# A two-layer hybrid block: the mLSTM value projection as seven products of quarters, with 4 KB slots and a matmul order that groups 128-column matmuls

## The chip, the cores and the metric

The kernel runs on one core of a Trainium2 chip. The metric is the device time of one execution in microseconds (us); lower is better. Five engines matter: TensorE (PE in the profile, its weight loads are PEld), VectorE (DVE), ScalarE (ACT), GpSimd (POOL), and SyncE (SP), which here only issues transfers.

## The reference, cut to what matters

Two layers of this (512 tokens, model width 1024, float32):

```python
h = rmsnorm(x, norm_g)
proj = h @ w_in            # aq, ak, av, az, bqk, bv, bi, bf, bo, bz, ga, gb
oa = diff_attention(rope(norm(aq)), rope(norm(ak)), av, lam)
ya = (rmsnorm(oa) * silu(az)) @ w_out_a
qk = silu(causal_conv(bqk))
hb = mlstm(q, k, bv, i_pre, f_pre)        # 8 heads, values 128 wide
yb = (sigmoid(bo) * rmsnorm(hb) * silu(bz)) @ w_out_b
u = sigmoid(ga) * ya + sigmoid(gb) * yb
x = x + u @ w_o
```

The piece changed most is `bv = h @ w_bv`, a product of 512 x 1024 by 1024 x 1024, whose result the mLSTM heads use as values.

## The kernel before

**Numbers.** Every float32 operand is cut in two: hi, rounded to the type that TensorE takes, and lo, the rest. ScalarE writes hi and VectorE subtracts to get lo (`split`). A product is three matmuls (`mm3`): hi by hi, hi by lo, lo by hi. `hh` and `hl` are hi and lo of the normalised input, transposed, resident for the whole layer.

**Pieces.** The weights come in pieces of 128 x 1024 (512 KB). For each, SP's queue loads `wr` (two buffers), `prep` splits it into `wh` and `wl` (three buffers each), and TensorE runs 24 matmuls of 512 columns. A token piece (qk, av, bv; `tok_piece`) adds into four accumulators, one for each 128 tokens; four pieces finish half the columns. A feature piece (az, bqk, bo, bz, ga, gb, woa, wob; `feat_piece`) finishes 128 columns in one accumulator. PSUM has four accumulators (`ps_acc`), a double one for scores (`ps_sc`), and one each for transposes and for head outputs. `TUNE["order"]` is the hand-written order of pieces.

**Seven products.** The output projection wo already runs as seven products of quarters (`seven`): both matrices are cut into 2 x 2 quarters, the products P1 to P7 take sums of quarters as operands, and their results are joined. A product is two pieces of 12 matmuls. Three accumulator pairs are used: X for P1, P6, P7, P4; Y for P5, P3; Z (the score accumulator) for P2. The sums on the weight side are made by loading one quarter on SP's queue and adding others in with accumulating transfers on POOL's queue (`add_up`). The sums on the other side are made from the gated rows by VectorE (`u_forms`).

**Heads.** Around these pieces, eight attention heads and eight mLSTM heads a layer run as chains of steps (`attn_head`, `ml_head`), timed in units of a quarter piece by offsets in TUNE. They need VectorE and ScalarE for masks, exponentials, norms and splits, and TensorE for scores, transposes and value products.

**The planner.** All instructions are first recorded, then `Recorder.schedule` orders them by a model of each engine: at each step the engine that can start earliest takes the candidate with the lowest key. A key is a due time, worked back from the order of TensorE's work, with offsets by tile name (`bias`), `slack`, `margin`, and penalties such as `drain`; `pemargin` is an extra delay before TensorE may use what another engine wrote. SP keeps program order. The result is a fixed order for each engine's queue; every queue runs in that order, and an instruction that waits holds those behind it.

**Memory.** Slots of 4 KB a partition (`qkp`, tag q2, 20 of them; `take` and `give` count them) hold hi-lo pairs, sums and forms. Besides, a 16 KB tile `big` holds in turn x, the q and k of attention groups 0 and 2, and `ua`.

Of the kernel before, what the change touches and what calls it, by code (L numbers as in the profile page):

```python
# [42 lines left out]
    ),  # L43
    "qkt": 5,
    "gct": 15,
    "gls": 6,
    "glf": 5,
    "attn": (1, 5, 5, 8, 9, 13, 15, 16, 19, 24),
    "a0": 23,
    "ap": 18,  # L50
    "a4": 7,
    "ml": (1, 9, 11, 12, 13, 28),
    "ahead": 3,
    "lc": 7,
    "slack": 4956.0,
    "margin": 72.0,
    "pemargin": 206.2,
    "wait": 333.1,
    "swpen": 141896579.9,
    "smargin": 51.6,  # L60
    "pwait": 0.7,
    "wdiff": 3673.3,
# [9 lines left out]
    "acl": 14,  # L72
    "gateA": 9,
    "gateM": 4,
    "actp": (0, 2, 3),
    "m0": 217,
    "mp": 15,
    "m4": 9,
    "slots": 20,
    "bias": {'av': 30400.0, 'msp_a': -4350.0, 'wl': 2200.0, 'wo': -3700.0, 'woh': -4650.0, 'ht': 29250.0, 'taz': -4050.0, 'ga': 25150.0, 'gt': -8800.0, 'p': -900.0, 'wo1_P': 27550.0, 'out_0_dram': -5850.0, 'p5_wo': -4950.0, 'rot': 12400.0, 'dq': -4400.0, 'oa': 450.0, 'dd': 31000.0, 'num': 20100.0, 'ld': -7300.0, 'ws1_wo': -2200.0, 'gw': -1100.0, 'hl': -600.0, 'sc': -1500.0, 'uz': -3750.0, 'mk': 7950.0, 'sbz': 4200.0, 'az': 12900.0, 'posi': 3200.0, 'msl_d': 1650.0, 's1_wo': 5000.0, 'msh_d': 6450.0, 'sq': -1400.0, 'warm': 3150.0, 'bo': -450.0, 'sdl': 150.0, 'ml': 16100.0, 'fo_b': 12850.0, 'ws0_wo': -900.0, 'wt1_wo': 1400.0, 'pb': 8800.0, 'sbo': 5350.0, 'qkt': 3900.0, 'junk': 7400.0, 'ulZ': 6400.0, 'bv': 650.0, 'bqk': -1750.0, 'uh': -3950.0, 'ms_b': -1100.0, 'ob': -400.0, 'uy': 1500.0, 'ms': 11100.0, 'ms_a': 1750.0, 'ones': 4150.0, 'msh_b': 8300.0, 'x1d': -3000.0, 'saz': 1000.0, 'xr': -3950.0, 'wo0_P': 450.0, 'qk1_0x': 2050.0, 'msh_a': 6050.0, 'rnh': -3150.0, 'gft': 6600.0, 'gct': 3100.0, 'kl': -700.0, 'qk1_2x': -800.0, 'gf': 1550.0, 'qk0_0x': -1600.0, 'qy': 7250.0, 'msl_a': 1400.0, 'x': -4550.0, 'eps': -600.0, 'wt0_wo': -2500.0, 'xn': 400.0, 'msl_b': 2150.0, 'rn': -400.0, 'glf': -3500.0, 'ss': 7600.0, 'sinv': 6150.0, 'ulA': -2650.0, 'epsc': -3000.0, 'ulB': 950.0, 'ulY': -300.0, 'tbz': 350.0, 'hh': 3700.0, 'fo_a': 6500.0, 'mx': -1800.0, 'gc': -150.0, 'mq': -1050.0, 'ang': 3150.0, 'qt': -2500.0, 'uhZ': -1250.0, 'em': -6800.0, 'ct': 1000.0, 'fo_d': 3850.0, 'par': -250.0, 'ks': 250.0, 'den': -400.0, 'sdh': -1000.0, 'cv': -300.0, 'ng': 3750.0, 'uhB': 300.0, 'rows': -300.0, 'zw': 50.0, 'qs': 1350.0, 'ctab': 950.0, 'gcol': 3400.0, 'ul': 1000.0, 'fb_b': 400.0, 'sums': 400.0, 'cosv': 250.0},  # L80
    "drain": 467.1,
    "risk": 268.4,
    "late": 912.7,
# [18 lines left out]

class Recorder:
# [3 lines left out]
    ACT_SET = {"Exp": (0, 6), "Tanh": (0,), "Ln": (6,), "Sin": (9,)}  # L107
    SET_NAME = {0: "exp_and_others", 6: "natural_log_exp_and_others", 9: "trig_and_small"}
# [56 lines left out]
    def add(self, eng, e, fn, a, k):  # L165
# [49 lines left out]
        self.ops.append({"eng": eng, "e": e, "fn": fn, "a": a, "k": k, "pre": preds, "cost": cost, "nom": self.pe_time, "rows": rows, "kind": a[0].tensor.name.rstrip("_0123456789")})  # L215
# [56 lines left out]
    def schedule(self):  # L272
# [48 lines left out]
        at_rows = {"ACT": (0, 0), "DVE": (0, 0)}  # L321

# [15 lines left out]
        while len(order) < n:  # L338
# [42 lines left out]
            if e in at_rows:  # L381
                if o["rows"] != at_rows[e]:
                    s = max(s, free[e] + 115.0)
                at_rows[e] = o["rows"]
            if e == "ACT":
# [59 lines left out]
def kernel(ctx, tc, x, pos, wp, wg, cst, par, pb, ngb, out):  # L445
# [53 lines left out]
    xcur = big.tile([P, NT, D], F32, tag="big", name="x0")  # L499
# [76 lines left out]
    state = {"x": [xcur[:, tt, :] for tt in range(NT)], "t": 0, "n": 0, "q2": 1}  # L576
# [9 lines left out]
    def run_due():  # L586
        fn = heapq.heappop(due)[2]
        if fn() is False:
            at(state["t"] + 1, fn)
# [36 lines left out]
    def layer_events(l):  # L626
        lam_init = 0.8 - 0.6 * math.exp(-0.3 * l)
        par_l = pt[l]
        st = {}
        xres = x if l == 0 else x1d  # L630
# [3 lines left out]
        def layer_consts():  # L634
# [26 lines left out]
            gc = cp.tile([P, 2], F32, tag=f"gc{l}", name=f"gc{l}")  # L661
            V.tensor_scalar(gc[:, 0:1], par_l[:, G_AN : G_AN + 1], 0.25 * (1.0 - lam_init), None, ALU.mult)
            V.tensor_scalar(gc[:, 1:2], par_l[:, G_MN : G_MN + 1], 0.125, None, ALU.mult)
            st["gc"] = gc


# [15 lines left out]
        def norm_scale(tt):  # L682
# [6 lines left out]
            if l:  # L689
                give(1)  # L690

        def norm_back(tt):
            if tt == NT - 1:
                give(1)
            junk = st[("junk", tt)]
            for hf in range(2):
# [8 lines left out]
                )  # L705

# [53 lines left out]
        CHAIN = {"P1": "X", "P6": "X", "P7": "X", "P4": "X", "P5": "Y", "P3": "Y", "P2": "Z"}  # L760
        LEFT = {"P1": "A00", "P2": "A01", "P3": "S4", "P4": "A11", "P5": "S1", "P6": "S2", "P7": "S3"}

        def seven(name, lhs, out, over):
            loc = {}
            seq = TUNE["prods"].split()

            def post(prod, t):
# [15 lines left out]
                elif prod == max("P3", "P6", key=seq.index):  # L783
                    out(0, 1, t, Y[t], X[t])
# [7 lines left out]
            def piece(prod, a):  # L792
                def run(wh, wl):
                    c = CHAIN[prod]
                    first = prod in ("P1", "P5", "P2")
                    if first and a == 0:
                        if prod == "P2":

                            z = ps_sc.tile([P, 2, S], F32, tag="sc", name=f"{name}{l}_{prod}")
# [12 lines left out]
                    if a == 1:  # L812
                        over(prod)
# [17 lines left out]

        def qk_done(c, tt, acc):
            if tt == 0:
                names = ("qs0", "qs1", "ks0", "ks1")
                if c % 2 == 0:
                    until(lambda: c == 0 or st.get(("A", 1), 0) > 5)
                    xt = big.tile([P, 8, S], F32R, tag="big", name=f"qk{l}_{c}x")
                    st[("qs", c)] = [xt[:, 2 * i : 2 * i + 2, :] for i in range(4)]
                    take(2)
                else:  # L840
                    take(6)
                    st[("qs", c)] = [q2(f"{n}{l}_{c}") for n in names]
                st[("kl", c)] = [half_zero(f"kl{r}{l}_{c}", r) for r in range(2)]
                st[("rq", c)] = cp.tile([P, NT, 8], F32, tag=f"rq{c % 2}", name=f"rq{l}_{c}")
            sq = t2(f"sq{l}_{c}_{tt}")
            if tt % 2 == 0:
                st["qss"] = small(16, f"qss{l}_{c}_{tt}")
            ss = st["qss"][:, 8 * (tt % 2) : 8 * (tt % 2) + 8]
# [22 lines left out]
            st[("rot", tt % 2)] = rq  # L871
# [3 lines left out]
            both = st["qss"]  # L875
# [9 lines left out]
            for t in (tt - 1, tt):  # L885
                qk_back(c, t, st[("rot", t % 2)])

        def qk_back(c, tt, rq):
# [5 lines left out]
            else:  # L894
                V.tensor_tensor(k3, k3, rk, ALU.mult)

# [17 lines left out]

        def v_done(tag):
            def f(c, tt, acc):
                take(1)
                v = q2(f"{tag}{l}_{c}_{tt}")
                st[(tag, c, tt)] = v
                split(v[:, 0, :], v[:, 1, :], acc)  # L920

            return f


        def silu2(dst, acc, name):
            t = t2(name)
# [3 lines left out]
        def az_done(m, acc):  # L930
            if m > 1:
                until(lambda: st.get(("A", m - 2), 0) > 9)
# [4 lines left out]
        def bo_done(m, acc):  # L937
            until(lambda: st.get(("A", 6 + m), 0) > 9 if m < 2 else st.get(("M", m - 2), 0) > 5)
# [11 lines left out]
        def ga_done(m, acc):  # L950
            if "ua" not in st:
                until(lambda: st.get(("A", 5), 0) > 5)
                st["ua"] = big.tile([P, 8, S], F32, tag="big", name=f"ua{l}")
            A.activation(st["ua"][:, m, :], acc, AF.Tanh, scale=0.5)
            st[("ua", m)] = st["ua"][:, m, :]
# [8 lines left out]
        def gb_done(m, acc):  # L964
            if m < 2:
                until(lambda: st.get(("M", 6 + m), 0) > 5)
# [4 lines left out]
        def wob_done(m, acc):  # L971
            n = st["nu"] = st.get("nu", -1) + 1
            g, u = st[("gb", m)], st["ua"][:, m, :]
            V.scalar_tensor_tensor(g, g, 1.0, acc, ALU.add, ALU.mult)
            V.tensor_tensor(u, g, u, ALU.add)
            st["ud", m] = True
# [669 lines left out]
```

## Time and profile before

| | |
|---|---|
| three runs | 1335.08, 1333.81, 1333.95 us; median 1333.95 |
| the profiled execution | span 1333.4 us, clock of TensorE 0.999 of full |
| ScalarE table loads | 65 of 1283 ns, 83.4 us |
| transfers | 148.15 MB, 111 GB/s on average; 138.63 MB on SP's queue, 8.39 MB on POOL's |
| stretches of layer 0 | attention to 325 us, woa from 312 to 416, mLSTM heads to 571, wob from 554 to 632, wo from 633 to 672 |
| bv in layer 0 | first half 269 to 301 us, second 469 to 494 us |

How to read it. The page gives each engine's busy time and share. The waits name for each engine whose instruction it waited for, with total, number and longest. The chain that ended last is followed back from the last instruction; an engine with nearly all of it sets the time. The groups put together all instructions with the same operation and tiles, with their busy time in us and mean length in ns, and after the second bar the idle time ahead of them. The windows give the busy time of each engine in a stretch. Matmuls overlap, so the length of one (about 390 ns for 512 columns) is not its price; the distance from start to start is. All instructions carry the same line (L441), because one helper issues them all, so tile names tell them apart. The second layer starts near 672 us and repeats the first, some 659 us later.

### The profile page before, as it was taken

Reading aid. Unit: us, or ns where it says so; the run is one execution under the profiler, and the core shown is the slowest. Engines: PE = TensorE matmul, PEld = TensorE weight load, DVE = VectorE, ACT = ScalarE, POOL = GpSimd, SP = SyncE. Lnnn points to the kernel's source line nnn. Section 1 sums busy time; section 2 is a strip of 40 time slices with the busy share of each in tenths; the row PEclk is TensorE's granted clock in tenths of the full one; section 3 lists DMA queues with packets and bytes.
Section 4 is the critical chain, followed back from the end, with each engine's and each line's share of the span. In section 5 each row is a group of like instructions: output and inputs, shape, how many; then the busy total and the mean of one; then the engine's idle time right before and its main releaser. Section 6 shows DMA issues by size and latency. Waiting matters only on the chain.

```text
span 1333.4 us, 17564 instructions
## 1 busy us (share of the span) xinstructions
PE 1326.1 (99%) x6200; PEld 1096.4 (82%) x6200; DVE 1018.1 (76%) x1846; ACT 907.4 (68%) x1836; POOL 37.0 (3%) x44
## 2 busy tenths in 40 slices
PE   8999999999999999999999999999999999999998
PEld 7888888888888888888888888888888888888887
DVE  7898899786259967755888988997852698687466
ACT  5878888877237958743667787888762478687243
POOL 1000000000000000000200000000000000000000
PEclk9999999999999999999999999999999999999999
DMA  5222222323344433544832121223232444345546
GB/s 188 87 65 79 80 80 64 95 79 94 100 121 124 119 114 109 154 148 123 258 125 88 49 96 54 89 67 92 82 110 81 123 134 124 98 129 148 170 123 181
DMA packets 51274, 148.15 MB, mean 111 GB/s; under 512 B 6097, under 2 KB 12881, under 8 KB 51185
## 3 DMA queue, kind: packets, MB, share of 16 engines
q1 hardware_dynamic: 48880, 138.63, 33.5%
q0 software_dynamic: 2304, 8.39, 3.5%
q8 instruction: 49, 0.80, 0.3%
q14 instruction: 41, 0.33, 0.1%
HBM read 142.74 MB, written 4.26 MB: 110 GB/s over the span
## 4 chain that ended last, share of the span: by engine, by line
PE 97%; ACT 1%; DVE 1%; DMA 0%; issue 0%; SPq 0%; DVEq 0%
PE qk L441 13%; PE av L441 9%; PE az L441 7%; PE bv L441 7%; PE bo L441 7%; PE bqk L441 7%; PE ga L441 7%; PE woa L441 7%; PE wob L441 7%; PE gb L441 6%; PE bz L441 6%; PE wo_P L441 6%; PE sc L441 3%; PE num L441 2%; PE ut L441 1%; PE ms L441 1%
## 5 line engine op out<-in xcount | busy, mean ns | idle before, releaser
L441 ACT CAST wh<-wr 128x1024 fp32r<-128x1024 f32 (+1 forms) x206 | 214.6, 1044 | 181.9 <-PE wob L441 41.0
L441 DVE TENSOR_TENSOR wl<-wr,wh 128x1024 fp32r<-128x1024 f32 (+1 forms) x208 | 249.0, 1200 | 107.1 <-ACT wh L441 106.3
L441 PE MATMUL qk<-wh,hh 128*128 128x512 f32 x256 | 96.8, 403 | 1.0 <-ACT hh L441 1.0
L441 PE MATMUL qk<-wl,hh 128*128 128x512 f32 x256 | 94.9, 397 | 0.5 <-DVE wl L441 0.5
L441 PE MATMUL qk<-wh,hl 128*128 128x512 f32 x256 | 94.9, 401 | 0.1
L441 ACT ACTIVATE p<-sc,mx,rq 128x128 f32<-128x128 f32 (+3 forms) x128 | 78.9, 619 | 18.5 <-DVE mx L441 17.8
L441 PE MATMUL woa<-oa,wh 128*128 128x512 f32 x256 | 86.4, 389 | 0.0
L441 PE MATMUL wob<-ob,wh 128*128 128x512 f32 x256 | 84.4, 389 | 0.0
L440 ACT ACT_TABLE_LOAD x65 | 83.4, 1283 | 1.1
L441 PEld LDWEIGHTS qk<-wh,hh 128*128 128x128 f32 x256 | 47.8, 189 | 11.1 <-ACT hh L441 1.3
L441 PEld LDWEIGHTS qk<-wl,hh 128*128 128x128 f32 x256 | 48.3, 189 | 9.9 <-DVE wl L441 0.9
L441 PEld LDWEIGHTS wob<-ob,wh 128*128 128x128 f32 x256 | 48.1, 188 | 10.1
L441 PEld LDWEIGHTS qk<-wh,hl 128*128 128x128 f32 x256 | 48.0, 189 | 9.9 <-DVE hl L441 0.4
L441 PEld LDWEIGHTS woa<-oa,wh 128*128 128x128 f32 x256 | 47.9, 188 | 9.9
L441 DVE TENSOR_REDUCE mx<-sc 128x2 f32<-128x256 f32 (+1 forms) x64 | 52.5, 820 | 1.1
L441 PE MATMUL bo<-hh,wl 128*128 128x512 f32 x128 | 50.3, 393 | 0.0
L441 PE MATMUL bo<-hh,wh 128*128 128x512 f32 x128 | 50.2, 392 | 0.0
L441 PE MATMUL bo<-hl,wh 128*128 128x512 f32 x128 | 50.2, 392 | 0.0
L441 PE MATMUL bqk<-hh,wl 128*128 128x512 f32 x128 | 50.0, 393 | 0.0
L441 PE MATMUL bz<-hh,wl 128*128 128x512 f32 x128 | 49.9, 393 | 0.0
L441 PE MATMUL bz<-hl,wh 128*128 128x512 f32 x128 | 49.9, 393 | 0.0
L441 PE MATMUL bz<-hh,wh 128*128 128x512 f32 x128 | 49.9, 392 | 0.0
(309 smaller groups left out, 3692.9 us busy)
## 6 DMA issues: line engine op xcount, KB each, us to landing
wr<-in_wp_dram SPq DMA_DIRECT2D x204, 512.0 KB, 3.6
ws_wo<-in_wp_dram POOLq DMA_DIRECT2D x12, 512.0 KB, 6.7
dd<-rows SPq DMA_DIRECT2D x16, 256.0 KB, 4.0
em<-rows SPq DMA_DIRECT2D x16, 256.0 KB, 3.9
dd<-rows SPq DMA_DIRECT2D x16, 192.0 KB, 5.0
x<-in_x_dram SPq DMA_DIRECT2D x4, 512.0 KB, 7.9
dd<-rows SPq DMA_DIRECT2D x16, 128.0 KB, 6.1
ws_wo<-in_wp_dram SPq DMA_DIRECT2D x4, 512.0 KB, 5.2
```

Source lines behind the costliest of these rows:

```text
L440: self.tc.keep_in_program_order(self.nc.scalar.preload_act_table_set(self.SET_NAME[o["load"]]))
L441: self.tc.keep_in_program_order(getattr(o["e"], o["fn"])(*o["a"], **o["k"]))
```

## The change

**bv as seven products.** In place of two halves of four token pieces, bv runs as P1, P5, P2, P3, P6, P7, then the piece bqk0, then P4, all behind the last woa piece. The left operands A00, A01 and A11 are read from `hh` and `hl`. The four sums on that side (S1 to S4) are built in mid-layer, six pieces ahead of P1: hi and lo are added up again and combined by eight operations of VectorE, and each is split just before its product.

```diff
+        def late_forms():
+            take(4)
+            fs = {}
+            for op in ("A10", "A11", "A00", "A01"):
+                x = fs[op] = q2w(f"lf{op}{l}", F32).rearrange("p (k t) -> p k t", k=4)
+                ks, ts = 4 * int(op[2]), 256 * int(op[1])
+                a, b = (st[w][:, ks : ks + 4, ts : ts + 256].bitcast(F32) for w in ("hh", "hl"))
+                V.tensor_tensor(x, a, b, ALU.add)
...
+                if op == "A00":
+                    s3 = fs["A10"]
+                    V.tensor_tensor(s3, x, s3, ALU.subtract)
+                    V.scalar_tensor_tensor(x, fs["A11"], -1.0, x, ALU.mult, ALU.subtract)
...
+        def h_reload(n, op):
+            if n in TUNE["lates"]:
+                if op in st["lf"]:
+                    take(2)
+                    src = st["lf"].pop(op)
+                    hi, lo = (q2w(f"l{w}{op}{l}").rearrange("p (k t) -> p k t", k=4) for w in "hl")
+                    split(hi, lo, src)
+                    give(1)
```

**Joins.** P2's join adds the copy of P1, P7's the copy of P5. At the later of P3 and P6, ScalarE copies Y and VectorE adds X to it. The results are split into v as before; the sign that comes out turned goes into the norm's constant (`gc`). While P2 runs, no head starts its scores.

```diff
                 elif prod == max("P3", "P6", key=seq.index):
-                    out(0, 1, t, Y[t], X[t])
+                    if name == "wo":
+                        out(0, 1, t, Y[t], X[t])
+                    else:
+                        yc = t2(f"yc_{name}{l}_{t}")
+                        A.copy(yc, Y[t])
+                        out(0, 1, t, X[t], yc)
...
+        def raw(acc, more):
+            if more is None:
+                return acc
+            V.tensor_tensor(more, acc, more, ALU.add)
+            return more
```

**Weight sums.** A sum can be made by VectorE from pieces already loaded (`tdve`): T2 of bv, and T3 of wo. The settings name T1 and T2 of wo too, but its new order P5 P1 P2 P6 P3 P7 P4 rules them out, and they stay with POOL's queue.

```diff
+        elif prod == "P3":
+            if on_dve(n, "T2"):
+                plus("ws")
+            if on_dve(n, "T3"):
+                plus("wt")
+        elif prod == "P6" and not on_dve(n, "T4"):
+            add_in(l, n, "ws", 1, 0, a)
```

**Weights without VectorE.** For az0, bo6, woa4 and wob5, POOL's queue loads the weights, ScalarE writes minus the rounded value, and an accumulating transfer adds the weights to it, which leaves lo.

```diff
+        take(2)
+        wh, wl = q2w(f"dh{i}"), q2w(f"dl{i}")
+        src = wp[l, KIDX[key]]
+        G.dma_start(wh, src)
+        A.activation(wl, wh.bitcast(F32), AF.Copy, scale=-1.0)
+        G.dma_start(wl, src, accum_op=ALU.add)
```

**Slots.** `big` gives up its 16 KB tile for x, q and k, and `ua`; these now take 4 KB slots, of which there are 24.

```diff
-    "slots": 20,
+    "slots": 24,
...
-    xcur = big.tile([P, NT, D], F32, tag="big", name="x0")
+    xcur = [qkp.tile([P, D], F32, tag="q2", name=f"x0_{tt}") for tt in range(NT)]
```

**Planner.** A TensorE candidate of the other kind (up to 128 columns, or more) gets 4190.8 ns on its key, so the order keeps to one kind for longer; entering the small kind costs 22 ns in the model.

```diff
+                    if e == "PE" and ops[i]["small"] != small:
+                        k += TUNE["group"]
...
-    "slack": 4956.0,
-    "margin": 72.0,
-    "pemargin": 206.2,
-    "wait": 333.1,
+    "slack": 3188.5,
+    "margin": 0.0,
+    "pemargin": 16.8,
+    "wait": 431.4,
...
-    "drain": 467.1,
+    "drain": 76.2,
+    "group": 4190.8,
...
-    "kact": (0, 2),
+    "kact": (0, 1, 2),
...
-    "foldA": (2, 3, 5),
-    "foldM": (0, 1, 2, 3, 4, 7),
-    "foldD": (0, 1, 2, 3, 4, 5, 6, 7),
+    "foldA": (2, 3, 5, 6, 7),
+    "foldM": (0, 1, 2, 3, 4, 5),
+    "foldD": (0, 1, 2, 4, 5, 7),
...
-    "actp": (0, 2, 3),
+    "actp": (0, 2),
```

The order of the other pieces, the offsets of the head chains and all of `bias` are new as well: three more ga pieces (seven of eight) and bqk5 stand ahead of the first woa piece, bqk7 and bqk1 move behind bv. `kact` and `actp` choose ScalarE or VectorE for a scaling; `foldA`, `foldM` and `foldD` list the heads whose sum over partitions is folded first, which needs one matmul instead of two. Other new branches (products for qk and av, a Silu table, spilled forms) are switched off by their settings.

More of the change, by code (lines that the diff above doesn't have):

```diff
@@ L81 @@
-    "drain": 467.1,
-    "risk": 268.4,
-    "late": 912.7,
+    "acl": 6,
+    "gateA": 8,
+    "gateM": 6,
+    "actp": (0, 2),
+    "m0": 220,
+    "mp": 13,
+    "m4": 9,
+    "slots": 24,
+    "hfd": 1,
+    "tset": (0, 18),
+    "silu": (),
+    "pmask": 0,
+    "dlo": ('az0', 'bo6', 'woa4', 'wob5'),
+    "dla": 7,
+    "groups": (),
+    "vkeep": (('av', 0), ('av', 1), ('bv', 0), ('bv', 1)),
+    "qspill": {},
+    "vl": {('av', 0): 50, ('av', 1): 140, ('bv', 0): 228, ('bv', 1): 272},
+    "tdve": {'bv': ('T2',), 'wo': ('T1', 'T2', 'T3')},
@@ L84 @@
+    "drain": 76.2,
+    "group": 4190.8,
+    "lates": ('bv',),
+    "risk": 192.1,
+    "late": 333.7,
 }
@@ L214, in add @@
             rows = tuple(x.offset // math.prod(list(x.tensor.shape)[1:]) for x in [a[0]] + ins[:1])
-        self.ops.append({"eng": eng, "e": e, "fn": fn, "a": a, "k": k, "pre": preds, "cost": cost, "nom": self.pe_time, "rows": rows, "kind": a[0].tensor.name.rstrip("_0123456789")})
+        small = eng == "PE" and math.prod(list(a[2].shape)[1:] if fn == "matmul" else list(a[0].shape)[1:]) <= P
+        self.ops.append({"eng": eng, "small": small, "e": e, "fn": fn, "a": a, "k": k, "pre": preds, "cost": cost, "nom": self.pe_time, "rows": rows, "kind": a[0].tensor.name.rstrip("_0123456789")})
     @staticmethod
@@ L384, in schedule @@
                 at_rows[e] = o["rows"]
+            if e == "PE":
+                if o["small"] and not small:
+                    c += 22.0
+                small = o["small"]
             if e == "ACT":
@@ L574, in rope_tables @@
         A.activation(flat(cosv), n, AF.Sin)
-    state = {"x": [xcur[:, tt, :] for tt in range(NT)], "t": 0, "n": 0, "q2": 1}
+    state = {"x": xcur, "t": 0, "n": 0, "q2": 1 + NT, "gp": 0, "sc": 0}
     due = []
@@ L586, in run_due @@
     def run_due():
-        fn = heapq.heappop(due)[2]
+        t, _, fn = heapq.heappop(due)
         if fn() is False:
-            at(state["t"] + 1, fn)
+            at(max(state["t"], t) + 1, fn)
     def until(done):
@@ L629, in layer_events @@
         st = {}
+        order = TUNE["order"].split()
+        seqs = {}
+        for n in order:
+            if "." in n:
+                seqs.setdefault(n.split(".")[0], []).append(n.split(".")[1])
         xres = x if l == 0 else x1d
@@ L695, in norm_back @@
             junk = st[("junk", tt)]
+            i, t = tt // 2, tt % 2
+            if groups:
+                take(1)
+                f = st["hf", i, t] = q2w(f"hf{l}_{i}{t}", F32)
             for hf in range(2):
@@ new lines, in h_reload @@
+        def h_reload(n, op):
[5 more added lines that the diff above has]
+                    split(hi, lo, src)
+                    give(1)
+                    st[op] = [hi, lo]
+                return
+            if st.get((op, "at"), 0) < group[n]:
+                take(2)
+                st[op] = []
+                for w in "hl":
+                    x = q2w(f"h{op}{w}{l}_{group[n]}")
+                    SY.dma_start(x.bitcast(F32), st[op, w])
+                    st[op].append(x.rearrange("p (k t) -> p k t", k=4))
+                st[op, "at"] = group[n]
@@ new lines, in h_half, with h_over, over @@
+        def h_half(op, k, t):
+            if op[0] == "A":
+                k, o = k + 4 * (op[2] == "1"), 256 * (op[1] == "1")
+                ts = slice(o + t * P, o + t * P + P)
+                return st["hh"][:, k, ts], st["hl"][:, k, ts]
+            return tuple(x[:, k, t * P : t * P + P] for x in st[op])
+        def h_over(n):
+            last = n in group and groups[group[n]][-1] == n
+            def over(prod):
+                if n in TUNE["lates"] and LEFT[prod][0] == "S":
+                    give(2)
+                if last and LEFT[prod][0] == "S":
+                    if group[n] == 0 and len(groups) > 1:
+                        h_spill(LEFT[prod])
+                    give(2)
+            return over
@@ L913, in qk_back, with v_out, f, v_put @@
             defer(TUNE["qkt"], back)
-        def v_done(tag):
[L916 to L920, printed above, removed]
-            return f
+        def v_out(tag):
+            def f(i, c, t, acc, more):
+                tt = 2 * i + t
+                src = raw(acc, more)
+                if (tag, c) in TUNE["vkeep"]:
+                    v_put(tag, c, tt, src)
+                    return
+                if more is None:
+                    src = t2(f"vr_{tag}{l}_{c}_{tt}")
+                    A.copy(src, acc)
+                d = dram.tile([P, S], F32, name=f"vd_{tag}{l}_{c}_{tt}")
+                SY.dma_start(d, src)
+                st["vd", tag, c, tt] = d
+            return f
+        def v_done(tag):
+            return lambda c, tt, acc: v_out(tag)(tt // 2, c, tt % 2, acc, None)
+        def v_put(tag, c, tt, src):
+            take(1)
+            v = q2(f"{tag}{l}_{c}_{tt}")
+            st[(tag, c, tt)] = v
+            split(v[:, 0, :], v[:, 1, :], src)
+        def v_load(tag, c, tt):
+            def f():
+                if ("vd", tag, c, tt) not in st or (tt and (tag, c, tt - 1) not in st) or not room(1 if tt else 4):
+                    return False
+                src = t2(f"vl_{tag}{l}_{c}_{tt}")
+                SY.dma_start(src, st["vd", tag, c, tt])
+                v_put(tag, c, tt, src)
+            return f
+        def take_gate():
+            until(lambda: state["gp"] < 2)
+            state["gp"] += 1
         def silu2(dst, acc, name):
+            if name[1:3] in TUNE["silu"]:
+                A.activation(dst, acc, AF.Silu)
+                return
             t = t2(name)
@@ L950, in ga_done @@
         def ga_done(m, acc):
[L951 to L955, printed above, removed]
+            if ("uap", m % 4) not in st:
+                take(1)
+                st["uap", m % 4] = q2w(f"ua{l}_{m % 4}", F32)
+            st[("ua", m)] = st["uap", m % 4][:, S * (m // 4) : S * (m // 4) + S]
+            A.activation(st[("ua", m)], acc, AF.Tanh, scale=0.5)
         def woa_done(m, acc):
@@ L1246, in need @@
             def need(i):
+                if i in (0, 1, 3, 5) and state["sc"]:
+                    return False
                 if i in (0, 1, 3, 5) and st.get(("qkn", c), 0) < (1, 2, 0, 3, 0, 4)[i]:
@@ L1396, in need @@
             def need(i):
-                if i == 0 and "gcol" not in st:
+                if i == 0 and "gcol" not in st or i in (2, 3) and state["sc"]:
                     return False
@@ L1407, in ml_head @@
             chain(("M", h), t0, TUNE["ml"], [decay, expm, scores, scores2, num, fin], need)
-        def tok(n, c, lhs, done):
-            return [tok_piece((n, c, kk), lhs, done) for kk in range(4)]
         def fp(n, m, rhs, done):
@@ L1428, in layer_events @@
         out_p = []
-        for n in TUNE["order"].split():
+        for n in order:
             out_p += ps.pop(n)
@@ L1490, in load @@
             _, n, prod, a = key
+            if LEFT[prod][0] == "S" and n != "wo":
+                layers[l][3]["reload"](n, LEFT[prod])
             if prod in ("P1", "P2", "P3"):
@@ L1554 @@
             load(i + a)
+        for a in range(3, TUNE["dla"]):
+            dload(i + a)
         for a in range(TUNE["acl"] + 1):
@@ L1562 @@
             state["t"] += 1
+        if i in loaded and loaded[i] is None and pieces[i][1][0] != "seven":
+            give(2)
     assert not due
```

288 lines of the change are left out of this document (196 added, 92 removed), and 8 rows, old and new, of the table TUNE.

## The prediction

> **What bounds the kernel now.** I read the page first, then who waited for whom on TensorE, then the end of the chain that ended last, then single groups of instructions. The page:
>
> ```profile
> span 1333.4 us, 17564 instructions
> ...
> PE 1326.1 (99%) x6200; PEld 1096.4 (82%) x6200; DVE 1018.1 (76%) x1846; ACT 907.4 (68%) x1836; POOL 37.0 (3%) x44
> ...
> PE 97%; ACT 1%; DVE 1%; DMA 0%; issue 0%; SPq 0%; DVEq 0%
> ```
>
> TensorE is busy for 1326.1 of 1333.4 us and makes 97% of the chain that ended last. A busy TensorE need not be a fast one, so the next views show whether it waits and at what pace it runs. All the waits of TensorE in the whole run:
>
> ```profile
> PE warm L441 <- DVE ml L441: 1.6, 1, 1.6
> PE qk L441 <- ACT hh L441: 1.0, 1, 1.0
> PE qk L441 <- DVE wl L441: 0.5, 1, 0.5
> PE ht L441 <- DVE junk L441: 0.3, 1, 0.3
> ```
>
> Four waits, 3.4 us together, all of them in the first microseconds (the warm-up, the first norm, the first weight piece). After that no other engine and no transfer ever holds TensorE. The pace, from the end of the chain, where the output projection runs alone:
>
> ```profile
> 1291.58 38.17 PE wo_P L441 x168
> 1329.75 0.02 issue
> ```
>
> 168 matmuls of 512 columns take 38.17 us, 0.2272 us each. This block is itself a product of the new kind (seven products of 24 matmuls), so it is the price of what bv becomes. The Trainium skill (TensorE: Matmul & The Clock Gate, section Back-to-back issue gap) gives about 131 ns for a 512-column matmul in a sustained stream of weight loads and matmuls; by that, 48 matmuls would be worth an estimated 6.3 us. This trace has 227 ns, and the measurement decides.
>
> **The change, part by part.** First, the matmuls removed. The groups of instructions have bv in three lines:
>
> ```profile
> L441 PE MATMUL bv<-wh,hl 128*128 128x512 f32 x128 | 46.9, 397 | 0.0
> L441 PE MATMUL bv<-wh,hh 128*128 128x512 f32 x128 | 46.8, 398 | 0.0
> L441 PE MATMUL bv<-wl,hh 128*128 128x512 f32 x128 | 45.2, 394 | 0.0
> ```
>
> 3 x 128 = 384 matmuls in two layers, 192 a layer. Seven products, each with 2 pieces, 2 row tiles, 2 steps of the contraction and 3 matmuls of hi and lo, are 168 a layer. 48 matmuls go, at 0.2272 us: **-10.9 us**. TensorE never waits after the start, so the whole of it comes off the end, if nothing else begins to hold it. The changed lists of folded heads move no sum: foldA gains two heads and foldD loses two, at one 512-column matmul each, and foldM keeps its count.
>
> Second, the grouping. A group of one transpose and a group of three, from the order of time on TensorE:
>
> ```profile
> 71.44 0.40 PE L441 MATMUL az<-hl,wh 128*128 128x512 f32 x1
> 71.67 0.49 PE L441 MATMUL ut<-ct,p 128*128 128x128 f32 x3
> 72.70 0.39 PE L441 MATMUL az<-hh,wl 128*128 128x512 f32 x1
> ...
> 241.74 0.39 PE L441 MATMUL ga<-hh,wl 128*128 128x512 f32 x1
> 241.97 0.27 PE L441 MATMUL ut<-ct,p 128*128 128x128 f32 x1
> 242.77 0.40 PE L441 MATMUL ga<-hh,wh 128*128 128x512 f32 x1
> ```
>
> Between the first and last start of each stand four matmuls of 512 columns (0.91 us). What is left is 0.35 us for three transposes and 0.12 us for one: a transpose costs about 0.115 us, and entering a group costs between nothing and 0.03 us. The code forms at most 118 batches of transposes (64 of ut, 32 of qkt, 16 of ht, 6 of the gates), so never splitting one again is worth 0 to 3.5 us. Most are short as they stand, so I take **-0.5 us**. A preference of 4.19 us for staying in one kind can also hold back a head's chain; that is in the rivals.
>
> Third, the work for the other engines. Its prices:
>
> ```profile
> L441 DVE TENSOR_TENSOR wl<-wr,wh 128x1024 fp32r<-128x1024 f32 (+1 forms) x208 | 249.0, 1200 | 107.1 <-ACT wh L441 106.3
> L441 ACT CAST wh<-wr 128x1024 fp32r<-128x1024 f32 (+1 forms) x206 | 214.6, 1044 | 181.9 <-PE wob L441 41.0 <-PE ga L441 37.0 <-PE woa L441 19.4
> L441 ACT COPY s_wo<-wo_P 128x512 f32<-128x512 f32 x4 | 2.3, 590 | 0.0
> L441 DVE TENSOR_TENSOR xr<-xr,s_wo 128x512 f32<-128x512 f32 x4 | 2.6, 691 | 0.0
> ```
>
> Per layer VectorE gets eight operations of 1024 elements that build the four forms (9.6 us), four lo parts of forms (4.8), six more lo parts of weights, 14 for 8 (7.2), two weight sums added by hand (2.4) and six adds that join two products (6 x 0.69 = 4.1). It loses four lo parts that the POOL queue now makes by transfers (4.8). That is 23.3 us a layer, 47 in all: 1018 becomes 1065 of about 1322 us, 81%. ScalarE gets ten hi parts (10.4) and six copies (3.5), 14 us a layer: 70%. The moves of single operations between the two (kact, actp) are a few us either way and lie in the attention stage. Where the new work falls decides; four stages:
>
> ```profile
> 10.00:220.00 210.00, 209.35 (x1017) 172.27 (x1018) 190.91 (x445) 169.26 (x476) 3.80 (x4) 0.99 0.27 83
> ```
> ```profile
> 312.00:399.00 87.00, 87.00 (x385) 72.05 (x384) 37.87 (x45) 34.24 (x46) 0.00 (x0) 1.00 0.34 104
> 399.00:571.00 172.00, 171.88 (x799) 142.99 (x798) 140.09 (x198) 132.35 (x187) 3.77 (x4) 1.00 0.44 124
> 633.00:669.00 36.00, 36.00 (x164) 29.83 (x163) 31.90 (x45) 23.24 (x34) 7.26 (x8) 1.00 0.82 247
> ```
>
> The columns are length, then busy time of PE, PEld, DVE, ACT, POOL. bv moves behind the last woa piece, into the stretch 312 to 399, where VectorE is busy 37.9 of 87 us and ScalarE 34.2. The new 23.3 us, and the 15.1 us that bv had before and brings along (eight lo parts at 1.20, eight splits at about 0.69), leave 10.7 us of the 87, and the stretch itself grows by most of the 38 us in which the products run. The attention stage (VectorE 191 of 210 us) gets lighter by half of bv and one bqk and heavier by three ga pieces, which cost VectorE only a lo part each. The mLSTM heads (140 of 172 us) lose the other half of bv, 7.6 us, and gain about one bqk. So the slack hides the new work; if the forms ran in the attention stage instead, 19 us of idle time in 210 would have to take them, and little of it would be left.
>
> Fourth, waits inside the seven products. They hold all four accumulators, so TensorE has little else to run while they last. That is the state of wo in 633 to 669: VectorE busy 31.9 of 36 us, and TensorE 36.00 of 36.00. In bv the copies of P1 and P5 have three and more products of cover, and P4 has bqk0 ahead of it. The tight place is P7 right behind P6: it adds onto the accumulator that the join of P6 still reads, with six matmuls (1.36 us) between, for a copy made earlier and an add of 0.69 us. A lo part of 1.2 us in the way would cost up to 0.6 us: 0 to 1.2 us in two layers, taken as 0.2 us.
>
> Fifth, the sums on the POOL queue. Its transfers of before:
>
> ```profile
> L441 POOL DMA_DIRECT2D ws_wo<-in_wp_dram x12: 865/865/1007, 561.9 to 1309.2; - x12
> ...
> DMA to landing us min/median/max: 4.4/6.1/9.0
> ```
>
> The sum for P4 is started when P6's first split is done. From there to P4 lie P6, P7 and bqk0, 72 matmuls or 16.4 us, against 0.9 of issue, at worst 9.0 to land, and 1.04 and 1.20 for the split: 12.1 us, hidden with 4 us to spare. Behind a waiting POOL instruction queue the other sums, the memsets of kl and mql, and now eight more transfers a layer for az0, bo6, woa4 and wob5, which wait for a free slot and for ScalarE; the sums are asked for six pieces ahead (32 us).
>
> Sixth, wo begins with P5, which needs the Y forms of the last gated rows (three adds and a split) where P1 needed a split alone. 12 to 24 matmuls cover it (2.7 to 5.5 us): 0 to 2 us a layer, taken as 0.3 us in all. The smaller slots (x, the q and k of even groups and ua now in 4 KB pieces of one pool) add no instruction; a late slot would appear as a wait of a DMA or of ScalarE.
>
> The sum against the profiled run: 1333.4 - 10.9 - 0.5 + 0.2 + 0.3 = 1322.5 us. The three runs shown have a median of 1333.95, 0.6 us above that span, so 1323.1, **1323 us**. The start (the four waits) and the tail (3.7 us behind the last matmul) stay.
>
> **The rivals.**
>
> A, slower: TensorE follows the other engines too closely. The planner used to place a TensorE instruction 206.2 ns behind the modelled end of its input, now 16.8 ns, with the general margin gone from 72 to 0. If real operations end later than modelled, each handover costs up to 0.19 us. 58 late handovers eat the 10.9 us; if one in two of the 208 weight pieces in the row above were late, 104 x 0.19 = 20 us, 1343 us. For it: no wait in 1320 us shows that the old margin sufficed, not that it was not needed. Against it: ScalarE's idle time before wh is ended by TensorE (wob, ga, woa), so weights are made as soon as a buffer is free, pieces ahead. Chance 0.13.
>
> B, half of it lost: the products of bv stall in mid-layer, at P5 or P3 for forms that VectorE made late, at P7 and P4 for reads behind a lo part. Two to four stalls of 1.2 us a layer, or one late form chain of 5 us: 5 to 10 us, 1328 to 1333. For it: nothing else can run then; against it, wo at 89% of VectorE without a wait. Chance 0.19, of which 0.05 lands within 0.2% of before.
>
> C, more than forecast: batches stay whole, and the small delays behind each group go too: 3 to 6 us more, 1317 to 1320. Chance 0.10.
>
> D, POOL sums land late. With 16.4 us of cover and 3.1 us for issue and split, a landing over 13.3 us starts to cost; a product (5.45 us) lost in each layer cancels the gain, 1334. The slowest landing was 9.0 us, with VectorE at 89%. The Trainium skill (SBUF — State Buffer, section SBUF: two separate sides, the "DVE blocks DMA" trap) says that VectorE operations which take the port shared with GpSimd keep it from writing the descriptors of POOL-queue transfers. In wo this did not show in the landings. Chance 0.03.
>
> **How the numbers follow.** The forecast (1320 to 1326.5) has 0.55. About 0.2%, 2.7 us, is what a measurement of this kernel can tell from no change. Faster by more: 0.55 + 0.10 + 0.14 of B = 0.79. Within: 0.05 of B and 0.02 of D = 0.07. Slower: 0.13 + 0.01 = 0.14. The range, 1317 to 1333.5 us, takes in C and B and leaves out A and D.
>
> **What would show it.** Right: 168 matmuls a layer for bv at 0.227 us, TensorE's waits still under 5 us in all, VectorE near 1065 us, landings on POOL below 13 us. Wrong: waits of TensorE on wl, on forms or on joins in bv's stretch (B), many short waits all over (A), or a busy TensorE that is no shorter by 11 us.

## The result, and the profile after

The change made the kernel slower: 1341.84 us median (1341.69 to 1345.95, 5 runs) against 1333.95 (1333.52 to 1335.08, 5 runs), ratio 1.0066, 95% interval [1.0054, 1.0079]. One execution in the experiments below (1449.02 us, at a mean clock of 0.851) was far slower than the others of its kernel and stands in no median. The profiled execution has a span of 1340.1 us (before: 1333.4). From its page:

```profile
span 1340.1 us, 17612 instructions
...
PE 1320.6 (99%) x6152; PEld 1084.7 (81%) x6152; DVE 1065.2 (79%) x1906; ACT 925.0 (69%) x1880; POOL 55.2 (4%) x68
...
PE 82%; DVE 6%; ACT 5%; DMA 5%; issue 2%; SPq 0%; DVEq 0%; ACTq 0%; POOLq 0%
```

The 48 matmuls are gone (6200 to 6152) and VectorE is busy as long as forecast. But of the chain that ended last only 82% is TensorE, where it was 97%. Span less busy time is TensorE's idle time: 7.3 us before, 19.5 after, so 12.2 more, while its busy time fell by 5.5 and not by 10.9. The longest waits of TensorE (engine, tile, whom it waited for; total us, number, longest). In an mLSTM head TensorE's `ms` are the scores and `den` the sum that divides them; VectorE and ScalarE make what these read, `mq`, `dd`, `fo_d` and `msh_d`:

```profile
PE den L469 <- ACT msh_d L469: 4.3, 2, 2.4
PE ms L469 <- ACT mq L469: 2.5, 2, 1.5
PE warm L469 <- DVE ml L469: 1.6, 1, 1.6
PE bv_P L469 <- DVE s_bv L469: 1.6, 2, 0.8
PE den L469 <- DVE fo_d L469: 1.1, 2, 0.7
PE wo_P L469 <- DVE wl L469: 0.9, 3, 0.3
PE wo_P L469 <- DVE xn L469: 0.8, 1, 0.8
PE wo_P L469 <- DVE xr L469: 0.8, 1, 0.8
PE bv_P L469 <- DVE yc_bv L469: 0.7, 1, 0.7
```

Apart from the warm-up these are 14 waits with 12.7 us, none of which existed before: 7.9 us in the mLSTM heads (den, ms), 2.5 in the output projection, 2.3 in the new products. They are few and long. The same by stretches, the products of bv, the mLSTM heads and wo of layer 0, then the mLSTM heads and wo of layer 1 (length, then busy time of PE, PEld, DVE, ACT, POOL):

```profile
345.00:397.00 52.00, 50.55 (x223) 41.12 (x221) 36.46 (x40) 27.66 (x35) 5.90 (x7) 1.00 0.58 153
399.00:571.00 172.00, 167.45 (x773) 137.38 (x772) 140.08 (x201) 132.57 (x188) 3.32 (x4) 1.00 0.43 116
634.00:674.00 40.00, 38.97 (x173) 31.51 (x172) 35.22 (x47) 23.39 (x34) 4.18 (x5) 1.00 0.79 246
1058.00:1230.00 172.00, 168.64 (x780) 138.40 (x779) 141.69 (x203) 133.54 (x191) 3.33 (x4) 1.00 0.43 120
1295.00:1337.00 42.00, 39.75 (x170) 30.94 (x168) 31.69 (x41) 16.67 (x21) 1.72 (x2) 1.00 0.60 184
```

The row 399 to 571 is the telling one. VectorE is busy for 140.08 us and ScalarE for 132.57, as before (140.09 and 132.35), yet TensorE stands for 4.55 us where it stood for 0.12. The load did not grow; the inputs come at the wrong time. The largest single wait, on ScalarE, TensorE and SP's queue (idle time before an instruction and what ended it in brackets):

```profile
541.60 1.05 ACT L469 CAST wh<-wr 128x1024 fp32r<-128x1024 f32 x1 [2.98 <-DMA wr<-in_wp_dram]
542.66 1.28 ACT L468 ACT_TABLE_LOAD   x1
543.96 0.63 ACT L469 ACTIVATE ms_b<-ms_b 128x512 f32<-128x512 f32 x1
544.49 0.60 ACT L469 CAST msh_d<-dd 128x512 fp32r<-128x512 f32 x1
```
```profile
542.38 0.39 PE L469 MATMUL bz<-hh,wl 128*128 128x512 f32 x1
545.15 0.50 PE L469 MATMUL den<-msh_d,ones 128*128 128x512 f32 x1 [2.37 <-ACT msh_d L469]
545.48 0.40 PE L469 MATMUL bz<-hh,wh 128*128 128x512 f32 x1
```
```profile
531.14 1.75 SPq L469 DMA_DIRECT2D dd<-rows  x4
535.30 0.33 SPq L469 DMA_DIRECT2D wr<-in_wp_dram  x1
```

A weight piece is sent at 535.30, as soon as VectorE has read the buffer's last piece (until 535.24), and behind four loads of rows. ScalarE can start on it at 541.60: 6.3 us, against a median landing of 3.6 us in the whole run. ScalarE stands for 2.98 us in front of `wh`; behind it in its queue are a table load, `ms_b` and `msh_d`; and TensorE has `den` next in its order and stands for 2.37 us, although it has other matmuls of bz to do. In the whole run ScalarE's waits for such pieces are 6.2 us in 5 before and 32.4 us in 19 after.

### The profile page after: what moved, and what is told of

Same layout as the page of the kernel before. It is cut to its first block, busy times and chain, and to the rows that moved or that the text cites. A ratio compares the mean times of both kernels' runs of the same rounds, so it can differ in the third digit from the quotient of the medians.

```text
span 1340.1 us, 17612 instructions
## 1 busy us (share of the span) xinstructions
PE 1320.6 (99%) x6152; PEld 1084.7 (81%) x6152; DVE 1065.2 (79%) x1906; ACT 925.0 (69%) x1880; POOL 55.2 (4%) x68
## 4 chain that ended last, share of the span: by engine, by line
PE 82%; DVE 6%; ACT 5%; DMA 5%; issue 2%; SPq 0%; DVEq 0%; ACTq 0%; POOLq 0%
PE qk L469 13%; PE av L469 9%; PE az L469 7%; PE ga L469 7%; PE woa L469 7%; PE wob L469 7%; PE gb L469 6%; PE bqk L469 5%; PE bv_P L469 4%; PE wo_P L469 4%; PE bz L469 3%; PE sc L469 3%; DMA wr<-in_wp_dram 3%; PE bo L469 2%; PE num L469 1%
## 5 line engine op out<-in xcount | busy, mean ns | idle before, releaser
L469 DVE TENSOR_TENSOR wl<-wr,wh 128x1024 fp32r<-128x1024 f32 (+1 forms) x196 | 233.8, 1197 | 35.4 <-ACT wh L469 34.4
L469 PE MATMUL wob<-ob,wh 128*128 128x512 f32 x224 | 70.9, 389 | 0.0
L469 ACT CAST ks<-qkt 64x256 fp32r<-64x256 f32 x128 | 47.0, 367 | 13.5 <-DVE qs L469 12.1
L469 PE MATMUL ga<-hl,wh 128*128 128x512 f32 x128 | 50.9, 398 | 0.0
L469 PE MATMUL ga<-hh,wl 128*128 128x512 f32 x128 | 50.5, 395 | 0.0
L469 PE MATMUL ga<-hh,wh 128*128 128x512 f32 x128 | 50.3, 393 | 0.0
L469 PE MATMUL bqk<-hh,wh 128*128 128x512 f32 x128 | 50.2, 392 | 0.0
L469 PE MATMUL gb<-hh,wh 128*128 128x512 f32 x128 | 50.0, 391 | 0.0
L469 PE MATMUL bqk<-hl,wh 128*128 128x512 f32 x128 | 50.0, 391 | 0.0
L469 PE MATMUL gb<-hl,wh 128*128 128x512 f32 x128 | 49.9, 390 | 0.0
```

The lines of the kernel that those rows point to most:

```text
L469: self.tc.keep_in_program_order(getattr(o["e"], o["fn"])(*o["a"], **o["k"]))
```

## The experiments

The first theory was that the seven products are worth their 48 matmuls (24 a layer), and that the new settings of the planner, which changed the order of every queue, lose more than that. Its rivals: the loss is in the products themselves, or it is the smaller margin that rival A named.

**The products taken out, all else new.**

```diff
-bv.P1 bv.P5 bv.P2 bv.P3 bv.P6 bv.P7 bqk0 bv.P4
+bv0 bv1 bqk0
```

> The changed kernel with bv back as two halves of four token pieces (bv0 bv1 bqk0 in the place of the products); all other settings stay, the planner orders anew. If the products are worth their 48 matmuls and the loss comes from the new planner settings (theory 1), the time is the changed kernel's 1341.8 + 10.9 - 3.4 (the waits at bv's own accumulators in two layers, which go) = about 1349 us, with TensorE's waits at den and ms of the mLSTM heads still there. If the products themselves bring the loss, by their load on VectorE, ScalarE and the queues (theory 2), those waits go and the time is 1334 to 1342 us.

Measured: 1350.44 us (1350.22 to 1351.31), ratio 1.0126 [1.0113, 1.0139]. The products save 8.6 us against this kernel, which has all the other settings of the change and no products, and which is 16.5 us slower than before. Its two longest waits in the mLSTM heads:

```profile
PE den L469 <- ACT msh_d L469: 3.6, 2, 1.9
PE ms L469 <- ACT mq L469: 2.1, 2, 1.0
```

The two longest kinds of waits are there without a single product. So the products are not what brings these.

**The margin alone.**

```diff
-    "pemargin": 16.8,
+    "pemargin": 206.2,
```

> The changed kernel with the extra delay before TensorE may use another engine's result back at 206.2 ns (16.8); nothing else, the planner orders anew. If the thin margin is what lets TensorE run into late inputs (rival A of the prediction), most waits after the start go and the time is 1330 to 1335 us. If the inputs are late by microseconds, because weight transfers land later than planned, 0.19 us covers none of them: 1340 us or more, with waits of 1 to 3 us on TensorE.

Measured: 1346.24 us (1344.89 to 1346.65), ratio 1.0092 [1.0079, 1.0105]: slower, not faster.

```profile
PE ms L469 <- DVE dd L469: 3.2, 2, 1.8
PE den L469 <- DVE fo_d L469: 2.1, 2, 1.4
```

The waits have moved to other tiles and are still microseconds long. A margin of 0.2 us doesn't cover inputs that are 1 to 2 us late, which speaks against rival A's mechanism.

**One false wait, orders kept.** In the products P2 fills both halves of one accumulator tile, and VectorE's read of one half was issued ahead of the last matmuls into the other, which then wait for that read (364 us, `s_bv`, 0.78 us). Here the read comes behind three of them:

```diff
+                        if isinstance(x, bass.AP) and x.tensor.name in z:
+                            pre[i] |= {j for j in z[x.tensor.name] if j < i}
...
+        order = self.replay(self.schedule(), 1, ())
```

> The changed kernel with every engine's order untouched; only VectorE's read of P2's first half is put down behind the first three matmuls of P2's other half that were recorded before it, in bv and in wo, so that these no longer wait for that read; the six matmuls after them still do. Theory: the four waits of 0.95 us at P2 come from this false wait; 0.68 us of each is then covered: 1341.8 - 2.7 = 1339 us. If VectorE's read was late for another reason, the time stays at 1342 us.

Measured: 1341.55 us (1338.80 to 1342.43, 5 runs), ratio 1.0051 [1.0039, 1.0064], not to be told from the change. TensorE's waits at P2 fell from 3.2 us (`s_bv` 1.6 in bv, `xn` and `xr` 0.8 each in wo) to 1.4 (`s_bv` 1.1, `xr` 0.3): the read starts later, and the next matmul behind the three waits for it. In wo other waits came, 0.7 us for `wh` and 0.3 more for `wl`. Inconclusive as to its 2.7 us; the place is real but small.

**TensorE's three latest steps moved back.** The matmuls of den of head 2, ms of head 6 and den of head 6 come 6, 9 and 13 matmuls later in TensorE's order, in both layers; the other queues are kept.

```diff
+        order = self.replay(self.schedule(), 0, (('den0_2_', 0, 6), ('ms0_6_', 0, 9), ('den0_6_', 0, 13), ('den1_2_', 0, 6), ('ms1_6_', 0, 9), ('den1_6_', 0, 13)))
```

> The changed kernel with all orders as they were but TensorE's: den of head 2, the six or so score matmuls of head 6 and den of head 6 stand 6, 9 and 13 matmuls later, in both layers. If TensorE's fixed order is the loss (it waits there with other matmuls at hand), the 8.9 us of waits at these six places become work: 1341.8 - 8.9 = 1333 us. If ScalarE and VectorE are the limit in this stretch, the heads end later by as much, the waits come back further on, and the time stays within 2 us of 1342.

Measured: 1349.82 us (1347.83 to 1350.93), ratio 1.0119 [1.0106, 1.0132]: 8 us slower, which neither theory expected. About 1.7 us of it is TensorE at a granted clock of 0.57 from 531 to 535 us (last section). From the orders of VectorE and ScalarE:

```profile
535.35 1.23 DVE L537 SCALAR_TENSOR_TENSOR dd<-ms,dd 128x1024 f32<-128x1024 f32 x1 [3.99 <-PE ms L537]
```
```profile
537.63 1.27 ACT L537 CAST sdh<-dd 128x1280 fp32r<-128x1280 f32 x1 [3.70 <-DVE dd L537]
```

VectorE now stands for 3.99 us on TensorE's `ms`, and ScalarE for 3.70 us on VectorE. TensorE's step was late for its input, and on time for its readers: there is no room on either side in these orders, and moving one queue handed the wait on.

The next theory, L: the piece that lands late is the cause, so a piece sent earlier cures it. Its rival, O: the orders are too tight whatever the transfers do. A third buffer for pieces needs 4 KB, so one slot goes; the first of the four runs is the control.

```diff
-    "slots": 24,
+    "slots": 23,
```

> The changed kernel with 23 slots of 4 KB instead of 24, planned anew; nothing else. It is the control for the next run, which needs the 4 KB. Both theories: the stalls stay where they are, 1339 to 1345 us.

Measured: 1346.86 us (1344.86 to 1347.73), 5 us over the change and above the 1339 to 1345 expected. One slot less, and another plan with other waits: each new plan moves the time by some us, which is the grain in which such runs, and the 8.6 us above, are to be read.

The third buffer, with every queue's order kept:

```diff
+            kw = {} if bufs is None else {"bufs": bufs + (tag == "raw")}
```

> Same order on every queue as the run with 23 slots, but the weight pieces that come by SP's queue get a third buffer, so that a piece may be sent for one piece (5.5 us) earlier; the planner is not told. Theory L (late pieces: the new order has no room for a piece that lands later than planned, ScalarE's queue stands still behind it, and VectorE and TensorE after it): ScalarE's waits for pieces fall from some 30 to under 8 us, TensorE's waits in the mLSTM stretch go, and the time falls by 8 to 15 us, to 1327 to 1334. Rival O (the order itself is too tight: operations of VectorE and ScalarE end later than planned, whatever the transfers do): within 3 us of the run with 23 slots.

Measured: 1354.55 us (1351.27 to 1354.85), 7.7 us slower than its control. The waits of ScalarE for pieces, and three of TensorE's:

```profile
ACT wh L469 <- DMA wr<-in_wp_dram: 15.4, 7, 2.8
```
```profile
PE msp_a L469 <- DVE fo_a L469: 4.2, 2, 2.2
PE den L469 <- ACT msh_d L469: 3.6, 2, 2.1
PE ms L469 <- ACT mq L469: 3.2, 2, 1.6
```

ScalarE's waits halved (31.6 to 15.4 us) and TensorE's did not: theory L falls as the sole cause. Some 6.5 us of this run is something else, TensorE at half its clock after four of the stalls (last section); what is left of the 7.7 lies within the 3 us of rival O.

The same with the two old halves in place of the products:

```diff
-bv.P1 bv.P5 bv.P2 bv.P3 bv.P6 bv.P7 bqk0 bv.P4
+bv0 bv1 bqk0
```

> The run with the third buffer, but with the value projection as the two old halves in place of the seven products, planned anew without knowledge of the buffer. If 48 matmuls a layer fewer are worth 10.9 us in a stretch where nothing else holds TensorE, it is slower than the run with the third buffer by 9 to 12 us. Theory L has it 8 to 15 us under the same edit without the buffer (1350.4), so 1336 to 1342; rival O has it at 1348 or more.

Measured: 1350.49 us (1348.53 to 1353.01), 4 us faster than with the products. Rival O's 1348 or more is met; that the halves would be 9 to 12 us slower is not. With its own plan it has other stalls, and half-clock stretches after one stall, not four. (The 48 matmuls of the expectation are those of both layers together.) The pair can't be used for the products' worth.

And the products with the third buffer, of which the planner now knows:

```diff
-                w = wpool.tile([P, 1024], F32, tag="raw", bufs=2, name=f"wr{i}")
+                w = wpool.tile([P, 1024], F32, tag="raw", bufs=3, name=f"wr{i}")
```

> Seven products, 23 slots, a third buffer for weight pieces, and the planner knows of it, so it may again plan closer. Theory L: at most a few us from the run where it doesn't know, 1325 to 1338, as pieces now have room anyway. Rival O: 1338 to 1346.

Measured: 1339.30 us (1339.13 to 1340.72), ratio 1.0039 [1.0025, 1.0054].

```profile
ACT wh L469 <- DMA wr<-in_wp_dram: 4.6, 3, 2.7
```

ScalarE's waits for pieces are back where they were before the change, and the time has come down by 2.5 us against the change, not by 10, and 2.5 us is less than the grain. Late pieces alone are at most a part of the loss; the time is O's.

**The output projection in its old order.**

```diff
-wo.P5 wo.P1 wo.P2 wo.P6 wo.P3 wo.P7 wo.P4
+wo.P1 wo.P5 wo.P2 wo.P6 wo.P3 wo.P7 wo.P4
...
-    "tdve": {'bv': ('T2',), 'wo': ('T1', 'T2', 'T3')},
+    "tdve": {'bv': ('T2',), 'wo': ('T3',)},
```

> The changed kernel with the products of the output projection in their old order (P1 before P5), T3 still by VectorE, planned anew. If the new order is what costs the 1.7 and 2.8 us in the two stretches of the output projection, TensorE's idle time there falls from 1.0 and 2.3 us to under 0.4 us each; if it is the late lo parts (too many operations of VectorE at the end of each layer), it stays over 0.7 us. The whole time is of less interest, as every stretch is planned anew: 1337 to 1346.

Measured: 1342.36 us (one run). The two stretches:

```profile
634.00:674.00 40.00, 40.00 (x180) 32.61 (x179) 34.95 (x47) 24.11 (x34) 5.91 (x7) 1.00 0.87 268
1296.00:1337.00 41.00, 40.39 (x176) 32.43 (x174) 32.57 (x41) 17.15 (x22) 3.45 (x4) 1.00 0.72 212
```

TensorE's idle time is 0.00 in layer 0 (1.03 in the change) and 0.61 in layer 1 (2.25), which is what the order theory asks for in the first and just above its bound in the second. The whole time has not moved, as other stretches got other waits.

**Room in the plan.** What is left is theory R (the arithmetic of the change is worth its matmuls, and only the orders lose it) against W (the change brings more work of the other engines than fits, in any order). The planner is told longer lengths, and its settings are chosen anew, for orders that stand when pieces land later still. This kernel and the next also have the third buffer and 23 slots:

```diff
-        cost = self.cost(eng, fn, a, k)
+        cost = self.cost(eng, fn, a, k) * (1.02 if eng in ("ACT", "DVE") else 1.0)
...
-                end[i] = max(dma, go) + 2000.0
+                end[i] = max(dma, go) + (2500.0 if e == "SP" else 2000.0)
...
-    "slack": 3188.5,
+    "slack": 2233.3,
...
-    "pemargin": 16.8,
+    "pemargin": 174.1,
```

Most of `bias`, some offsets of the head chains and the places of neighbouring pieces change with them; products, transfers and the engines of every operation don't (part of the edit is shown).

> The changed kernel with all its features (seven products, the grouping, weights and sums by the same engines), with a third buffer for weight pieces and 23 slots, and an order planned with more truthful lengths: transfers of SP's queue land 0.5 us later in the plan, operations of VectorE and ScalarE last 2% longer, and the settings of the planner (offsets, biases, order of neighbouring pieces) were chosen for an order that stands even when pieces land later still. Theory R (the products are worth their matmuls; the loss is an order that leaves no room for late inputs): TensorE's waits fall to some 5 us, and the time is 1321 to 1329. Rival W (the change brings more work of VectorE, ScalarE and the queues than fits beside TensorE, whatever the order): over 1334.

Measured: 1326.09 us (1324.39 to 1326.29), ratio 0.9935 [0.9923, 0.9948]: 15.8 us under the change and 0.65% faster than before.

> As the run before, with the value projection as the two old halves and settings chosen for that in the same way and the same time. Theory R: 9 to 12 us above the run before, the price of 96 matmuls less what 35 operations of VectorE and ScalarE spare; so 1330 to 1340. Rival W: not above it by more than 5 us.

Measured: 1336.44 us (1335.88 to 1338.53), ratio 1.0019 [1.0011, 1.0028]. The two old halves, planned in the same way, are 10.35 us slower than the products, and no better than the kernel before. (The 96 matmuls of the expectation are 48; its price is that of 48.) With the halves such a plan brings nothing over the kernel before; the gain comes with the products, as far as one chosen plan for each can say.

> As the run with room, but with two buffers for weight pieces and 24 slots as in the changed kernel, settings chosen in the same way: only the planner's lengths and settings differ from the changed kernel. Theory R: 0 to 6 us above the run with the third buffer, 1322 to 1333, and clearly under the changed kernel. If the buffer alone makes the difference: 1336 or more.

Measured: 1324.90 us (1323.29 to 1325.74), ratio 0.9929 [0.9916, 0.9943]. It differs from the change in the planner's lengths and settings alone (the places of neighbouring pieces and a margin of 123.9 ns among them), and is 16.9 us faster. It is also 1.2 us under the kernel with three buffers, where R had it 0 to 6 us above: the third buffer isn't needed. With two buffers ScalarE's waits for pieces are down to 5.6 us in 2, so the late pieces too came with the orders. Its page and its longest waits:

```profile
span 1322.0 us, 17622 instructions
...
PE 1312.7 (99%) x6152; PEld 1088.1 (82%) x6152; DVE 1064.0 (80%) x1906; ACT 923.2 (70%) x1880; POOL 55.3 (4%) x68
...
PE 95%; DMA 2%; DVE 1%; ACT 1%; issue 0%; SPq 0%; DVEq 0%; ACTq 0%
```
```profile
PE warm L469 <- DVE ml L469: 1.6, 1, 1.6
PE qk L469 <- DVE hl L469: 0.7, 1, 0.7
PE bv_P L469 <- DVE s_bv L469: 0.7, 2, 0.3
PE qk L469 <- ACT hh L469: 0.6, 1, 0.6
PE wo_P L469 <- ACT wh L469: 0.4, 1, 0.4
PE msp_b L469 <- DVE fo_b L469: 0.3, 1, 0.3
```

The same 6152 matmuls, VectorE busy for as long (1064.0 against 1065.2 us), and TensorE busy for 1312.7 us instead of 1320.6, idle for 9.3 instead of 19.5. Of the waits of the mLSTM heads one of 0.3 us is left (`msp_b`), and that stretch runs nearly full:

```profile
395.00:565.00 170.00, 169.68 (x792) 141.75 (x791) 142.33 (x205) 136.36 (x194) 3.32 (x4) 1.00 0.45 121
1050.00:1222.00 172.00, 172.00 (x802) 143.85 (x801) 144.84 (x207) 137.32 (x195) 3.32 (x4) 1.00 0.43 121
```

R holds and W falls: the same instructions, with the same load on every engine, fit in another order. Which of the two, the longer lengths or the new settings, does how much was not tried apart, and no new choice of settings under the old lengths was run. So that the orders lose the time is shown; that it is the room in them, and not only a better choice, is argued.

## Why the prediction was wrong

**The matmuls removed (-10.9 us): right.** 10.35 us between the kernels with room, where TensorE is busy for 1312.6 us against 1323.2, and 8.6 between the change and the change without products. The sum of the prediction, 1322.5 for the profiled execution, is near the last kernel's span, 1322.0, in part by luck: TensorE is busy there for 13.4 us less than before, where the sum has 11.4, and idle for 9.3, where it has 7.8.

**The step that failed** is the sentence after it: "TensorE never waits after the start, so the whole of it comes off the end, if nothing else begins to hold it." That TensorE never waited was a property of the old orders, and the change replaces the order of all queues. The third step then looked for room in shares of busy time ("So the slack hides the new work"). Its work was sized right (1065.2 us for 1065), and the shares in the mLSTM stretch did not move (the prediction had VectorE 7.6 us lighter there, less one bqk), but 32 us of idle VectorE in 172 say nothing about whether `msh_d` is there when its turn comes. In orders that are fixed, one piece 2 to 3 us late stops ScalarE, then TensorE, which can't run the matmuls behind.

**Rival A was in the right place with the wrong price.** It named an order that follows the other engines too closely, with 1343 us. But it priced many handovers at 0.19 us each; there were 14 waits with 12.7 us, the longest 2.4, and the kernel with the margin put back alone took 1346 us. Behind the first 30 us, TensorE's starts that waited for another engine and came 0.05 us or more late without leaving idle time are no more than before, 47 against 51, with 3.9 us in each. So its 1343, next to the measured 1341.84, is luck. It was put aside with "weights are made as soon as a buffer is free, pieces ahead". That row was of the old order, too: after the change ScalarE waits for pieces 19 times.

**Waits inside the products (0 to 1.2 us, taken as 0.2): too small.** P7 behind P6 did wait, 0.7 us in one layer; the larger wait, 1.6 us in two, stood at P2, whose halves share a tile, and had no place in the sum. With room in the plan they are 0.7 us in all.

**The output projection from P5 on (0 to 4 us, taken as 0.3): too small, and for another reason.** The waits of 2.5 us lie within the bounds by luck. None is for the Y forms that P5 reads: 1.6 us (`xn`, `xr`) stand at P2, as in bv, and 0.9 are for lo parts of weights. The old order removes most. The kernel with two buffers and room keeps P5 first and waits 0.4 us there.

**The sums on POOL's queue: right.** Median landings of 7.1 to 9.3 us for all of them, the slowest of bv 11.7, under the 13 at which they would cost. **The grouping (-0.5 us)** was not measured by itself; the halves with room have TensorE busy for 2.9 us less than before at the same 6200 matmuls (1323.2 against 1326.1), by grouping, folds and plan together.

Of TensorE's loss, 12.2 us is idle time in the views. The rest is 5.4 us of busy time that did not go away. A record lasts 0.39 us and the next matmul may start after 0.227, so up to 0.16 us of each wait counts as busy; and the first matmul behind a wait is followed after 0.33 us (545.15 to 545.48 in the view of `bz` and `den`). Added up over the waits behind the first 30 us, this is 4.0 us, against 0.6 before. So 3.4 of the 5.4 belong to the same waits, and 2.0 stay open.

## What to carry to other kernels

A fixed order that runs without waits shows that this order fits, not that there is room: when a change comes with a new order, ask how late each input may be before the engine that matters stops, and compare the plan's lengths with the landings in the trace. Test the arithmetic and the order apart, by running the old arithmetic in the new order, and both in orders chosen the same way. A queue whose step is late and whose readers are just in time was not cured here by moving that one step.

## What the runs showed of the hardware

TensorE's clock fell to about half after some waits, and stayed there for some 3 us. In the run with the third buffer, around the wait at 531 us (the column behind POOL is the granted clock):

```profile
531.00:534.00 3.00, 1.40 (x7) 0.87 (x6) 2.34 (x4) 2.88 (x6) 0.00 (x0) 0.97 0.00 0
534.00:538.00 4.00, 4.00 (x13) 3.26 (x12) 2.53 (x3) 2.41 (x5) 0.00 (x0) 0.60 0.31 84
538.00:542.00 4.00, 4.00 (x20) 3.37 (x19) 3.63 (x5) 2.82 (x4) 0.00 (x0) 1.00 0.80 73
```
```profile
532.99 0.67 PE L469 MATMUL ms<-mq,mk 128*128 128x384 f32 x2 [1.60 <-ACT mq L469]
534.28 0.73 PE L469 MATMUL gb<-hh,wh 128*128 128x512 f32 x1
534.81 0.63 PE L469 MATMUL gb<-hl,wh 128*128 128x512 f32 x1
535.24 0.63 PE L469 MATMUL gb<-hh,wl 128*128 128x512 f32 x1
```

The wait was 1.60 us; from 534.81 on the matmuls behind it start 0.43 us apart instead of 0.227. At the mean clock of 0.60 the four microseconds hold 2.4 us of work, so 1.6 us is lost on top of the wait. This run has it four times, behind the stalls at 308, 531, 975 and 1213 us; the run with the three steps moved back has it once, at 532 us, the changed kernel's profile not at all. There a wait of 2.37 us was followed by full clock (1.00 from 543 to 550 us), so length alone doesn't decide, and what does stays open. The Trainium skill (TensorE: Matmul & The Clock Gate, section HAM oscillation — how this bites in real kernels) warns of idle gaps over about 3.4 us; here the clock fell behind a gap of 1.60 us.
